# Value projection of the retention by seven products with stationary tokens, and the retention in a staggered, written-out order

## The chip, the cores and the metric

The kernel runs on one core of a Trainium2 chip. The metric is the time of one execution on the device, in microseconds. The work is spread over TensorE (PE in the rows: the matmuls; PEld its weight loads), VectorE (DVE), ScalarE (ACT), GpSimd (POOL), and SyncE (SP), which here only issues DMAs; ScalarE issues the stores, in its own order of instructions.

## What is computed

One decoder layer over 1024 tokens of 1024 channels. The part that the change touches is the retention branch: four heads with keys of 128 and values of 256 channels, in chunks of 128 tokens.

```python
h = rms_norm(x, norm_mix[l])
proj = h @ w_in[l]
aq, ak, av, rq, rk, rv, rg, ga, gr = jnp.split(proj, offsets, axis=-1)
...
def step(state, inp):
    qi, ki, vi = inp
    scores = jnp.einsum('bihd,bjhd->bhij', qi, ki) * decay_intra
    o = jnp.einsum('bhij,bjhv->bihv', scores, vi)
    o = o + jnp.einsum('bihd,bhdv->bihv', qi, state) * decay_q
    state = decay_chunk * state + jnp.einsum('bjhd,bjhv->bhdv', ki * decay_k, vi)
    return state, o
...
ret = head_group_norm(ret, ret_gn_gain[l]).astype(x.dtype) * jax.nn.silu(rg)
merged = jax.nn.sigmoid(ga) * (att @ w_att_o[l]) + jax.nn.sigmoid(gr) * (ret @ w_ret_o[l])
x = x + merged @ w_out[l]
h = rms_norm(x, norm_ffn[l])
x = x + (jax.nn.silu(h @ w_gate[l]) * (h @ w_up[l])) @ w_down[l]
```

`rv` is a product of 1024 tokens, 1024 channels in and 1024 out (four heads of 256); `k` is scaled by `dk ** -0.5` = 128 ** -0.5.

## The kernel before

The activations lie with channels on the partitions and tokens along the free side, in tiles of 128 x 512 (`ut`, 70 of them in a ring; a tile is free again when its last reader is done). Each float32 operand is split into a high and a low part (`split`: a cast on ScalarE, a difference `low` on VectorE), and a product is three matmuls, high x high, high x low, low x high (`mm3`). The normalized input is held in `hT` as high and low parts without the tokens' root mean square; `bc1` (a row per token, spread over the partitions) and `rn` (a column per token) put that in behind the product. Results land in eight banks of PSUM: four of `bank`, four of `abank`.

The stages follow one another: attention's projections and attention itself, with the gate projections `gr` and part of `ga` as filler; then the rest of `ga`, interleaved with attention's output product `ao` (`wo`, `m1`); then the retention; then rg, the product with `w_ret_o`, and the merge; the o stage; and the feed-forward part. The order on TensorE is the order in which the program is written, everywhere. In the feed-forward part, in the o stage and in the merge the other engines' order is written out too; in the stages from the start to rg it is made by a scheduler from what is ready.

The o stage already computes its product (merged with `w_out`) by seven products in place of eight: operands are cut into quarter blocks, sums of blocks (`four_sums`; for the weights `weight_sums`, stored in `d_WS`) are made ahead and stored, and seven products of 4 steps with 12 matmuls each (`o_mm`, `o_evac`), in the order of `STAGES`, reload them a few steps ahead.

Of the retention, the rows name these. `rqk_chunk` makes q or k of one head for 512 tokens (24 matmuls of 512 columns, weights stationary). `rv_chunk` makes the values of one head for 256 tokens: 2 x 8 x 3 = 48 matmuls of 256 columns with the tokens stationary, evacuated as high and low part (`rvh` on ScalarE, `rvl` on VectorE). One **unit** is one head and half of the tokens: `r1` (transposes `pk`, scores `rs`; `kn`, `sT`, `qd` on the other engines), `r2a` (state matmuls `rst`, the states and their parts `shl`), `r2b` (outputs `ro`, their statistics `bst`, `mv`, a root on GpSimd, the normalized `y`), `r3` (transposes `yt`, stored in `d_on`). All q, k and v of head 0 come first; then the units run, and between their steps a chunk of the next head's q, k, v fills TensorE, in the last head the first eight chunks of rg:

```python
for half in range(NH):
    r1(h, half)
    fl.pop(0)()
    r2a(h, half)
    fl.pop(0)()
    r2b(h, half)
    fl.pop(0)()
```

## Time and profile before

| what | value |
|---|---|
| runs | 1482.34, 1483.69 and 2457.64 us, median 1483.69 |
| profiled execution | 1482.5 us |
| its span in the trace | 1480.7 us |
| TensorE, VectorE, ScalarE, GpSimd busy | 1462.5, 972.3, 551.8, 105.8 us |
| matmuls | 7284 |
| DMA | 218.65 MB, mean 148 GB/s |

The span is what lies between the first and the last instruction; the execution's time is 1.8 us more. Busy times of different engines lie beside each other. A matmul's own time overlaps that of the next.

### The profile page before, as it was taken

How to read it: one execution, taken by the hardware profiler on the slowest of the kernel's cores; microseconds unless marked ns; L12 is line 12 of the kernel's file. 1: busy time of each engine (PE TensorE's matmuls, PEld its weight loads, DVE VectorE, ACT ScalarE, POOL GpSimd, SP SyncE). 2: the span in 40 equal slices, each digit the busy share in tenths (PEclk: the TensorE clock that was granted, in tenths of full speed). 3: DMA queues.
4: the chain of work that ended last, by engine and by line, in shares of the span. 5: the costliest groups of instructions: out<-in, count | busy, mean ns of one | idle time of the engine just before them, and what ended most of it. 6: DMA issues, size and time to landing. Idle time of an engine off the chain costs nothing.

```text
span 1480.7 us, 19756 instructions
## 1 busy us (share of the span) xinstructions
PE 1462.5 (99%) x7284; PEld 1239.5 (84%) x7284; DVE 972.3 (66%) x1762; ACT 551.8 (37%) x1055; POOL 105.8 (7%) x108
## 2 busy tenths in 40 slices
PE   9999999999999999999999999999999999999997
PEld 6888888888998998888878778888888888888887
DVE  5888876433445546634579798876667777568774
ACT  6554453211223324332255553222333325444441
POOL 6200000000010010000012300000000000010121
PEclk9999999999999999999999999999999999999999
DMA  5222114453112113345689334432334546799773
GB/s 198 87 66 71 64 44 137 145 166 124 46 45 72 44 43 99 115 147 187 234 275 328 101 104 152 136 124 103 106 126 157 172 161 208 259 323 369 222 234 110
DMA packets 108258, 218.65 MB, mean 148 GB/s; under 512 B 12225, under 2 KB 22593, under 8 KB 108161
## 3 DMA queue, kind: packets, MB, share of 16 engines
q1 hardware_dynamic: 77088, 161.91, 33.8%
q10 hardware_dynamic: 30656, 54.67, 10.0%
q8 instruction: 57, 0.93, 0.3%
q0 software_dynamic: 416, 0.81, 0.2%
q14 instruction: 41, 0.33, 0.1%
HBM read 158.88 MB, written 58.46 MB: 147 GB/s over the span
## 4 chain that ended last, share of the span: by engine, by line
PE 90%; DVE 5%; DMA 2%; issue 2%; ACT 1%; SPq 0%; POOL 0%; POOLq 0%; DVEq 0%; ACTq 0%
PE d L932 14%; PE fu L932 13%; PE fg L932 12%; PE o L932 3%; PE rv_p L102 2%; PE rv_p L104 2%; PE rv_p L103 2%; PE rg_p L102 2%; PE rg_p L103 2%; PE ga_p L102 2%; PE ga_p L103 2%; PE ga_p L104 2%; PE rg_p L104 2%; PE ro_p L102 2%; PE ro_p L103 2%; PE ro_p L104 2%
## 5 line engine op out<-in xcount | busy, mean ns | idle before, releaser
L128 POOL TENSOR_TENSOR ssq<-ssq,sq 128x512 f32<-128x512 f32 x39 | 61.1, 1566 | 788.3 <-DMA rt<-d_X 460.6
L102 PE MATMUL rv_p<-wrv_h,z_h 128*128 128x256 f32 x256 | 72.9, 285 | 0.0
L104 PE MATMUL rv_p<-wrv_h,z_l 128*128 128x256 f32 x256 | 72.4, 283 | 0.0
L103 PE MATMUL rv_p<-wrv_l,z_h 128*128 128x256 f32 x256 | 72.4, 283 | 0.0
L102 PE MATMUL gr_p<-z_h,wgr_h 128*128 128x512 f32 x128 | 50.7, 396 | 0.0
L102 PE MATMUL rg_p<-z_h,wrg_h 128*128 128x512 f32 x128 | 50.2, 392 | 0.0
L102 PE MATMUL ga_p<-z_h,wga_h 128*128 128x512 f32 x128 | 50.0, 391 | 0.0
L103 PE MATMUL gr_p<-z_l,wgr_h 128*128 128x512 f32 x128 | 49.9, 390 | 0.0
L104 PE MATMUL gr_p<-z_h,wgr_l 128*128 128x512 f32 x128 | 49.9, 390 | 0.0
L103 PE MATMUL ga_p<-z_l,wga_h 128*128 128x512 f32 x128 | 49.8, 389 | 0.0
L104 PE MATMUL rg_p<-z_h,wrg_l 128*128 128x512 f32 x128 | 49.8, 389 | 0.0
L103 PE MATMUL rg_p<-z_l,wrg_h 128*128 128x512 f32 x128 | 49.8, 389 | 0.0
L104 PE MATMUL ga_p<-z_h,wga_l 128*128 128x512 f32 x128 | 49.8, 389 | 0.0
L102 PE MATMUL ro_p<-reh,wro_h 128*128 128x512 f32 x128 | 49.8, 389 | 0.0
L103 PE MATMUL ro_p<-rel,wro_h 128*128 128x512 f32 x128 | 49.8, 389 | 0.0
L104 PE MATMUL ro_p<-reh,wro_l 128*128 128x512 f32 x128 | 49.8, 389 | 0.0
L103 PEld LDWEIGHTS rv_p<-wrv_l,z_h 128*128 128x128 f32 x256 | 49.1, 192 | 0.0
L102 PEld LDWEIGHTS rv_p<-wrv_h,z_h 128*128 128x128 f32 x256 | 49.1, 192 | 0.0
L104 PEld LDWEIGHTS rv_p<-wrv_h,z_l 128*128 128x128 f32 x256 | 49.1, 192 | 0.0
L974 ACT ACTIVATE fg_c<-fg_c 128x512 f32<-128x512 f32 x33 | 20.9, 633 | 71.7 <-DVE fg_c L1016 43.6
L852 ACT CAST fg_w_h<-fg_s 128x512 fp32r<-128x512 f32 x44 | 26.9, 619 | 53.2 <-PE fu L932 49.6
L852 ACT CAST fu_w_h<-fu_s 128x512 fp32r<-128x512 f32 x44 | 26.7, 615 | 45.4 <-PE fu L932 21.3
(1540 smaller groups left out, 4596.7 us busy)
## 6 DMA issues: line engine op xcount, KB each, us to landing
dr<-in_w_down_dram SPq DMA_DIRECT2D x56, 256.0 KB, 4.7
d_X<-fg_c ACTq DMA_DIRECT2D x44, 256.0 KB, 3.3
rt<-d_X SPq DMA_DIRECT2D x44, 256.0 KB, 4.5
x<-in_xT_dram SPq DMA_DIRECT2D x32, 256.0 KB, 5.4
rb<-d_X SPq DMA_DIRECT2D x32, 256.0 KB, 3.9
dr<-d_S SPq DMA_DIRECT2D x24, 256.0 KB, 4.0
fg_rb<-in_w_gate_dram SPq DMA_DIRECT2D x11, 512.0 KB, 4.0
fu_rb<-in_w_up_dram SPq DMA_DIRECT2D x11, 512.0 KB, 3.8
```

The source lines that it names most:

```text
L102: nc.tensor.matmul(ps, lhsT=wh, rhs=xh, start=start, stop=False)
L103: nc.tensor.matmul(ps, lhsT=wh, rhs=xl, start=False, stop=False)
L104: nc.tensor.matmul(ps, lhsT=wl, rhs=xh, start=False, stop=stop)
L128: nc.gpsimd.tensor_tensor(out=acc, in0=acc, in1=sq, op=ALU.add)
L852: nc.scalar.copy(out=hi, in_=src)
L932: nc.tensor.matmul(ps, lhsT=w[a][:, c], rhs=x, start=start and j == 0 and i == 0, stop=stop and j == len(xs) - 1 and i == 2, skip_group_ch ...
L974: nc.scalar.activation(s, t, AF.Silu)
```

## The change

The value projection is made once for all heads, as one product of 1024 x 1024 x 1024 by seven products of quarter blocks in the manner of the o stage. The tokens are the stationary side, 512 columns of weights move: 7 products x 4 blocks of 128 tokens x 4 blocks of channels x 3 = 336 matmuls of 512 columns (`h_mm`, 28 steps of 12).

- **Preparation**, in the stage of ga and ao: `h_in` loads x again (16 tiles), `h_blocks` normalizes them on VectorE, forms sums by `four_sums` and stores all seven kinds of blocks in `d_H`; `sums_load` and `sums_add` form the sums of the value weights (now laid out as quarters, `w_mix`) into `d_WM`. The sums of `w_out`, which stood there, move into the last 16 half-runs of rg.
- **q and k of head 0** come before the seven products (`rqk_p`), and are stored (`d_qk`) and loaded again.
- **The seven products** reload blocks (`h_load`, `hw_raw`), cut them (`h_hi`, `h_lo`, `hw_hi`, `hw_lo`), and add results up (`h_evac`); the values go to `d_v`. What each step of work is given ahead stands in a table `hat` by step.
- **The retention** gets its values from `d_v` (`r0`, cut in `r0v`). Its units are staggered: state matmuls of unit u, fill, output transposes of u-1, fill, scores of u+1, outputs of u, two fills. A fill is half a run of q, k (heads 1 to 3) or rg, 12 matmuls of 512 columns (`two_runs`, `pop`). The order on VectorE, ScalarE, GpSimd and SyncE is written out from here on as well. The states have five buffers in place of two, `ro` lies in `bank`, the products of rg with the retention's outputs are made later (`rg_fin`, `rg_end`), and `wro0` is loaded four half-runs before the end.
- The scale of k moves into the constants.

```diff
+    d_H = dr.tile([7, KD // 2, P, HT], F32, name="d_H")
+    d_WM = dr.tile([KD // 2, 4, P, HT], F32, name="d_WM")
+    d_qk = dr.tile([2, NH, P, HT], F32, name="d_qk")
+    d_v = dr.tile([NB, 2, P, HT], F32, name="d_v")
...
+    SUMS = ((1, 0, 1, 0), (0, 0, 2, 2), (2, 1, 2, 1), (3, 2, 3, 3))
+
+    def sums_load(src, name):
+        t = [ut(f"{name}{i}") for i in range(4)]
+        for i in range(4):
+            nc.sync.dma_start(t[i], src[:, i * 512:(i + 1) * 512])
+        return t
+
+    def sums_add(t, dst, i, put=None):
+        o, x, y, n = SUMS[i]
+        nc.vector.tensor_tensor(out=t[o], in0=t[x], in1=t[y], op=ALU.add)
+        (put or (lambda f: f()))(lambda: store(dst[n], t[o]))
+
+    def weight_sums(src, dst, name):
+        t = sums_load(src, name)
...
+    def h_in(j):
+        for r in range(2):
+            for c in range(NH):
+                t = ut(f"hn{2 * j + r}{c}")
+                nc.sync.dma_start(t, xv[2 * j + r, c])
+                HB_[j, r, c] = t
+
+    def h_blocks(j):
+        B_ = {}
+        for r in range(2):
+            for c in range(NH):
+                t = HB_.pop((j, r, c))
+                nc.vector.scalar_tensor_tensor(out=t, in0=t, scalar=gmix_s[:, 2 * j + r:2 * j + r + 1], in1=bc1[c],
+                                               op0=ALU.mult, op1=ALU.mult)
+                B_[r, c] = t
+        put = lambda q, t, d=0: store(d_H[QN.index(q), j], t)
+        for q, rc in (("b11", (0, 0)), ("b21", (1, 0)), ("b22", (1, 1))):
+            put(q, B_[rc])
+        HR["b11", j] = B_[0, 0]
+        h_hi("b11", j)
+        h_lo("b11", j)
+        one, two = four_sums(lambda r, c: B_[r, c], put, lambda i: ut(f"h{i}s{j}"))
+        two(one())
...
+    def hw_raw(k, i):
+        t = wp.tile([P, 1024], F32, tag="raw", name=f"hw{k}{i}_r", bufs=2)
+        if k in (1, 2, 4):
+            c = {1: 2, 2: 3, 4: 1}[k] * HT
+            src = w_mix[i:i + 2, :, c:c + HT]
+        else:
+            src = d_WM[i:i + 2, {5: 0, 6: 1, 7: 2, 3: 3}[k]]
+        nc.sync.dma_start(t.rearrange("p (i c) -> p i c", i=2), src.rearrange("i p c -> p i c"))
...
+    def h_mm(k, q, i):
+        if k not in (2, 3):
+            HB[{1: 2, 5: 3}.get(k, k), i] = HB[k, i] = (bank if k in (1, 5) else abank)(f"h{k}_{i}")
+        ps = HB[k, i]
+        ts = slice(i * P, (i + 1) * P)
+        for j in range(NJ):
+            xh, xl = HX[q][j]
+            wh, wl = HW[k, j][:2]
+            for n, (x, w) in enumerate(((xh, wh), (xh, wl), (xl, wh))):
+                nc.tensor.matmul(ps, lhsT=x[:, ts], rhs=w, start=k not in (2, 3) and j == 0 and n == 0,
+                                 stop=j == NJ - 1 and n == 2, skip_group_check=True)
...
+    def h_evac(k, i):
+        tt = nc.vector.tensor_tensor
+        ps = HB[k, i]
+        if k in (1, 2):
+            t = ut(f"hc{k}{i}")
+            nc.scalar.copy(out=t, in_=ps)
+            if k == 1:
+                HN[i] = t
+            else:
+                h_keep(0, 0, i, t)
+        elif k == 6:
+            tt(out=HN[i], in0=ps, in1=HN[i], op=ALU.subtract)
+        elif k == 7:
...
+    h_in(0)
+    NGB = 2 * KD
     for b in range(KD):
         for half in range(NH):
-            if 2 * b + half >= NGA:
+            if NGA <= 2 * b + half < NGB:
                 ga_chunk(b, half)
             if half == 0:
                 wo = wload(w_att_o[b], f"wao{b}")
@@ -484,44 +638,152 @@
             m1 = ut(f"m1{b}{half}")
             nc.vector.tensor_tensor(out=m1, in0=po, in1=SG.pop((b, half)), op=ALU.mult)
             store(d_m1[b, half], m1)
-        if b % 2:
-            weight_sums(b // 2)
-
-
+            if half == 0 and b % 2 == 0:
+                h_blocks(b // 2)
+            if half == 0 and b % 2 == 1 and b // 2 + 1 < NJ:
+                h_in(b // 2 + 1)
+            if half == 1 and b % 2 == 0:
+                WQ = sums_load(w_mix[b // 2], f"wq{b}")
+            if half == 0 and b % 2 == 1:
+                for i in range(4):
+                    sums_add(WQ, d_WM[b // 2], i)
+    for i, u in enumerate((U_RQ, U_RK)):
+        w = wload(w_in[u], f"wr{i}")
+        for half in range(NH):
+            ps = proj_half(w, hT, half, KD, f"rqk_p{i}{half}")
+            t = ut(f"rqk{i}{half}")
+            times_rstd(t, ps, half)
+            store(d_qk[i, half], t)
+            if i:
+                hw_raw(1, 2 * half)
+                for j in (2 * half, 2 * half + 1):
+                    hw_hi(1, j)
+                    hw_lo(1, j)
...
+    hsteps, hat = [], {}
+
+    def hahead(k, f):
+        hat.setdefault(max(k, 0), []).append(f)
+
+    for n, (k, q) in enumerate(STAGES):
+        for i in range(4):
+            t = 4 * n + i
+            if n > 0:
+                if i % 2 == 0:
+                    hahead(4 * n - 6 + i // 2, lambda a=(k, i): hw_raw(*a))
+                hahead(4 * n - 3 + i // 2, lambda a=(k, i): hw_hi(*a))
+                hahead(4 * n - 2 + i // 2, lambda a=(k, i): hw_lo(*a))
+                hahead(4 * n - 8 + i, lambda a=(q, i): h_load(*a))
+                hahead(4 * n - 6 + i, lambda a=(q, i): h_hi(*a))
+                hahead(4 * n - 5 + i, lambda a=(q, i): h_lo(*a))
+            hsteps.append((lambda a=(k, q, i): h_mm(*a), lambda a=(k, i): h_evac(*a)))
...
+            wat.setdefault(i - 8, []).append(lambda: w_in_raw(key, b, w_in[unit + b]))
+            wat.setdefault(i - 3, []).append(lambda: w_in_cut(key, b))
+
+        def run(a):
+            if a == 0:
+                run.ps = bank(f"{key}_p{b}{half}")
+            wh, wl = W[key, b][:2]
+            for k in range(4 * a, 4 * a + 4):
+                c = slice(k * P, (k + 1) * P)
+                mm3(run.ps, wh[:, c], wl[:, c], *hT[k][half], k == 0, k == KD - 1)
+            if a:
+                use(b, half, run.ps)
+
+        fl.extend([lambda: run(0), lambda: run(1)])
...
+    def rg_use(b, half, ps):
+        s = ut(f"srg{b}{half}")
+        times_rstd(s, ps, half)
+        soon.append(lambda: nc.scalar.activation(s, s, AF.Silu))
+        RS[b, half] = s
+
+    def rg_fin():
+        for b, half in [x for x in RS if (x[0] // 2, x[1]) in RD]:
+            s = RS.pop((b, half))
+            on = ut(f"onr{b}{half}")
+            nc.sync.dma_start(on, d_on[b, half])
+            later.append((2, lambda s=s, on=on, b=b, half=half: rg_end(s, on, b, half)))
+
+    def rg_end(s, on, b, half):
+        nc.vector.tensor_tensor(out=s, in0=s, in1=on, op=ALU.mult)
+        hl = ut(f"reh{b}{half}", F32R), ut(f"rel{b}{half}", F32R)
+        nc.scalar.copy(out=hl[0], in_=s)
+        later.append((1, lambda: low(hl[1], s, hl[0])))
+        ret[b][half] = hl
...
+    def retention_fill():
+        for h in range(1, 4):
+            for w, u in (("q", U_RQ), ("k", U_RK)):
+                for half in range(NH):
+                    two_runs("r" + w, u, h, half, rqk_use(w))
+        for c in range(2 * KD):
+            two_runs("rg", U_RG, c // 2, c % 2, rg_use)
+
...
+    def r0(h, half):
+        for i, w in enumerate("qk"):
+            if h == 0:
+                t = ut(f"r{w}{h}{half}")
+                nc.sync.dma_start(t, d_qk[i, half])
+                RT[w, h, half] = t
+        for c2 in (2 * half, 2 * half + 1):
+            t = ut(f"rv{h}{c2}")
+            nc.sync.dma_start(t.rearrange("p (t c) -> p t c", t=2),
+                              d_v[2 * c2:2 * c2 + 2, h // 2, :, (h % 2) * 256:(h % 2 + 1) * 256].rearrange("t p c -> p t c"))
+            RT["v", h, c2] = t
+
+    def r0v(h, half):
+        for c2 in (2 * half, 2 * half + 1):
+            hl = ut(f"rvh{h}{c2}", F32R), ut(f"rvl{h}{c2}", F32R)
+            split(RT["v", h, c2], *hl)
+            RT["v", h, c2] = hl
 
...
+    un = [(h, half) for h in range(4) for half in range(NH)]
+    NR = len(fl)
...
+    WS_ = []
+    for m in range(4):
+        wat.setdefault(NR - 16 + 3 * m, []).append(wm_sums(m))
+        for i in range(4):
+            wat.setdefault(NR - 16 + 3 * m + 2 + i // 2, []).append(
+                lambda m=m, i=i: sums_add(WS_[m], d_WS[m], i, lambda f: later.append((1, f))))
+    wat.setdefault(NR - 4, []).append(lambda: MWRO.append(wload(w_ret_o[0], "wro0")))
+    MWRO = []
...
+    def pop(n=1):
+        for _ in range(n):
+            i = ran[0]
+            ran[0] += 1
+            due = [f for d, f in later if d <= 1]
+            later[:] = [(d - 1, f) for d, f in later if d > 1]
+            for f in due + wat.pop(i, []):
+                f()
+            if fl:
                 fl.pop(0)()
-            r3(h, half)
-            if h < 3:
-                fl.pop(0)()
-    for f in rest[8:]:
-        f()
...
+    r0(*un[0])
+    r0(*un[1])
+    pop()
+    r0v(*un[0])
+    pop()
+    r1(*un[0])
+    pop(2)
+    for u in range(len(un)):
+        if u + 2 < len(un):
+            r0(*un[u + 2])
+        r2a(*un[u])
+        if u + 1 < len(un):
+            r0v(*un[u + 1])
+        pop()
+        if u > 0:
+            r3(*un[u - 1])
+            RD.add(un[u - 1])
+        pop()
+        if u + 1 < len(un):
+            r1(*un[u + 1])
+        rg_fin()
+        r2b(*un[u])
+        pop(2)
+    pop(1)
+    r3(*un[-1])
+    RD.add(un[-1])
+    rg_fin()
+    while fl:
+        pop(1)
+        rg_fin()
+    while later or wat:
+        pop()
+    hman.close()
 
...
+        dt[:, h] = np.where(diff >= 0, np.exp(lg * np.maximum(diff, 0.0)), 0.0) * P ** -0.5
         dq[:, h] = np.exp(lg * (idx + 1.0))[None, :]
-        dk[:, h] = np.exp(lg * (P - 1.0 - idx))
+        dk[:, h] = np.exp(lg * (P - 1.0 - idx)) * P ** -0.5
```

TensorE where the value projection begins, before (names: `z` channels of the normalized input, `wrk`, `wrv` weights, `_h` and `_l` high and low part):

```order
L102 MATMUL rk_p01_3337<-z71_h_356,wrk0_h_3305 128x512
L103 MATMUL rk_p01_3337<-z71_l_357,wrk0_h_3305 128x512
L104 MATMUL rk_p01_3337<-z71_h_356,wrk0_l_3306 128x512
L102 MATMUL rv_p00_3376<-wrv00_h_3365,z00_h_135 128x256
L103 MATMUL rv_p00_3376<-wrv00_l_3366,z00_h_135 128x256
L104 MATMUL rv_p00_3376<-wrv00_h_3365,z00_l_136 128x256
L102 MATMUL rv_p00_3376<-wrv00_h_3365,z10_h_144 128x256
```

And TensorE at the same place now (`hw` weights, `Hb11` the first block of tokens and channels, `h1_0` the bank of the first product's first token block):

```order
L107 MATMUL rqk_p11_3468<-z71_l_361,wr1_h_3427 128x512
L108 MATMUL rqk_p11_3468<-z71_h_360,wr1_l_3428 128x512
L595 MATMUL h1_0_3535<-hw10_h_3462,Hb110h_2579 128x512
L595 MATMUL h1_0_3535<-hw10_l_3463,Hb110h_2579 128x512
L595 MATMUL h1_0_3535<-hw10_h_3462,Hb110l_2580 128x512
L595 MATMUL h1_0_3535<-hw10_h_3462,Hb111h_2700 128x512
L595 MATMUL h1_0_3535<-hw10_l_3463,Hb111h_2700 128x512
```

Ahead of the projection stand q and k of head 0 in both, and the moving side of a matmul of the projection is now 512 columns in place of 256.

SyncE's queue in the stage of ga and ao, before (`wao`, `wga` weights of ao and ga, `ws` quarters of `w_out`):

```order
L86 DMA wga3_r_2696<-in_w_in_dram 128x1024
L86 DMA wao3_r_2730<-in_w_att_o_dram 128x512
L86 DMA wga4_r_2812<-in_w_in_dram 128x1024
L471 DMA ws00_2614<-in_w_out_dram 128x512
L471 DMA ws01_2615<-in_w_out_dram 128x512
```

And SyncE's queue in the same stage now (`hn` the x loaded again, `wq` quarters of the value weights):

```order
L528 DMA hn30_2643<-in_xT_dram 128x512
L528 DMA hn31_2645<-in_xT_dram 128x512
L90 DMA wga4_r_2882<-in_w_in_dram 128x1024
L90 DMA wao4_r_2916<-in_w_att_o_dram 128x512
L509 DMA wq20_2758<-in_w_mix_dram 128x512
```

wga4 stood behind wao3; now twelve loads of hn and wq, of which the last two are shown, have moved between them.

VectorE in the first unit of the retention, from its first state on, before (`wrq2` weights of q of head 2, `bst` the statistics of `ro`):

```order
L568 COPY state00_3662<-rst000_3655 128x256
L570 SCALAR_TENSOR_TENSOR state01_3667<-state00_3662,rst000_3655 128x256
L77 TENSOR_TENSOR shl00_3664<-state00_3662,shl00_3664 128x256
L570 SCALAR_TENSOR_TENSOR state02_3679<-state01_3667,rst001_3672 128x256
L77 TENSOR_TENSOR shl01_3669<-state01_3667,shl01_3669 128x256
L570 SCALAR_TENSOR_TENSOR state03_3684<-state02_3679,rst001_3672 128x256
L77 TENSOR_TENSOR shl02_3681<-state02_3679,shl02_3681 128x256
L77 TENSOR_TENSOR shl03_3686<-state03_3684,shl03_3686 128x256
L239 TENSOR_TENSOR rq11_3714<-rq_p11_3689,bc11_118 128x512
L77 TENSOR_TENSOR wrq2_l_4221<-wrq2_r_4219,wrq2_h_4220 128x1024
L596 BN_STATS bst0000_3728<-ro000_3716 128x6
L596 BN_STATS bst0001_3731<-ro000_3716 128x6
```

And VectorE at the same place now (`rvl` the low part of the values of the unit that follows):

```order
L831 COPY state00_4297<-rst000_4290 128x256
L833 SCALAR_TENSOR_TENSOR state01_4299<-state00_4297,rst000_4290 128x256
L833 SCALAR_TENSOR_TENSOR state02_4308<-state01_4299,rst001_4301 128x256
L833 SCALAR_TENSOR_TENSOR state03_4310<-state02_4308,rst001_4301 128x256
L81 TENSOR_TENSOR shl00_4312<-state00_4297,shl00_4312 128x256
L81 TENSOR_TENSOR shl01_4314<-state01_4299,shl01_4314 128x256
L81 TENSOR_TENSOR shl02_4316<-state02_4308,shl02_4316 128x256
L81 TENSOR_TENSOR shl03_4318<-state03_4310,shl03_4318 128x256
L81 TENSOR_TENSOR rvl02_4325<-rv02_4186,rvh02_4324 128x512
L81 TENSOR_TENSOR rvl03_4329<-rv03_4188,rvh03_4328 128x512
L81 TENSOR_TENSOR wrq2_l_4192<-wrq2_r_4190,wrq2_h_4191 128x512 x2
L243 TENSOR_TENSOR rk10_4365<-rk_p10_4336,bc10_121 128x512
```

The four states stand together, their low parts behind them, and then the low parts of the next unit's values, which came from the value projection's evacuation before; the statistics of `ro` come after the next unit's scores.

## Rows read from the trace of the kernel before

**Rows 1.** The profile's page: engines' busy time, and the chain that ended last
```profile
PE 1462.5 (99%) x7284; PEld 1239.5 (84%) x7284; DVE 972.3 (66%) x1762; ACT 551.8 (37%) x1055; POOL 105.8 (7%) x108
...
PE 90%; DVE 5%; DMA 2%; issue 2%; ACT 1%; SPq 0%; POOL 0%; POOLq 0%; DVEq 0%; ACTq 0%
```

**Rows 2.** Windows by stage: busy us (instructions) of five engines, clock, DMA share, GB/s
```profile
245.00:343.60 98.60, 98.60 (x436) 81.64 (x435) 37.84 (x50) 17.88 (x24) 0.00 (x0) 1.00 0.48 157
...
365.40:441.60 76.20, 76.20 (x554) 72.23 (x553) 34.11 (x70) 20.39 (x36) 6.26 (x10) 1.00 0.14 44
441.60:562.00 120.40, 120.40 (x839) 112.45 (x838) 60.52 (x127) 35.75 (x63) 12.50 (x20) 1.00 0.18 57
562.00:705.00 143.00, 143.00 (x678) 120.00 (x677) 75.62 (x130) 46.57 (x76) 4.99 (x9) 1.00 0.42 138
...
746.00:816.00 70.00, 69.00 (x310) 56.44 (x309) 60.47 (x91) 36.88 (x64) 13.51 (x9) 1.00 0.91 313
```

**Rows 3.** Costliest groups of the page: busy us, mean ns of one, idle before
```profile
L102 PE MATMUL rv_p<-wrv_h,z_h 128*128 128x256 f32 x256 | 72.9, 285 | 0.0
...
L102 PE MATMUL rg_p<-z_h,wrg_h 128*128 128x512 f32 x128 | 50.2, 392 | 0.0
```

**Rows 4.** Timeline of TensorE at three places: start us, length us, instruction
```profile
354.49 0.39 PE L102 MATMUL rk_p<-z_h,wrk_h 128*128 128x512 f32 x1
...
365.37 0.28 PE L102 MATMUL rv_p<-wrv_h,z_h 128*128 128x256 f32 x1
...
388.41 0.60 PE L535 MATMUL pk<-ident,rk 128*128 128x128 f32 x4
388.84 1.06 PE L538 MATMUL rs<-rq,rk 128*128 128x128 f32 x8
...
395.21 0.28 PE L102 MATMUL rst<-rvh,kn_h 128*128 128x256 f32 x1
...
410.10 1.04 PE L613 MATMUL yt<-ident,y 128*128 128x128 f32 x8
```

**Rows 5.** Groups of VectorE and ScalarE in the o stage, 746 to 816 us
```profile
L77 DVE TENSOR_TENSOR ow_l<-or,ow_h 128x512 fp32r<-128x512 f32 x26 | 19.7, 767 | 5.4 <-ACT ow_h L852 5.2
...
L852 ACT CAST ow_h<-or 128x512 fp32r<-128x512 f32 x24 | 14.8, 620 | 8.1 <-DMA or<-in_w_out_dram 5.5 <-DMA or<-d_WS 1.3
...
L793 ACT COPY on<-o 128x512 f32<-128x512 f32 x4 | 2.3, 584 | 0.0
```

**Rows 6.** Timeline of ScalarE: the issue of one store on its queue
```profile
742.89 0.33 ACTq L246 DMA_DIRECT2D d_M<-m1r  x1
```

**Rows 7.** Waits in the o stage: total us, times, longest us
```profile
ACT Mt41h L746 <- DMA mrt<-d_M: 2.4, 1, 2.4
...
PE o L932 <- DVE Mb213l L77: 0.5, 1, 0.5
```

**Rows 8.** Groups of VectorE in the retention, 441 to 562 us
```profile
L603 DVE TENSOR_SCALAR y<-ro,mv,rs 128x256 f32<-128x256 f32 x16 | 8.0, 540 | 7.6 <-POOL rs L600 7.6
L596 DVE BATCH_NORM_STATS2 bst<-ro 128x6 f32<-128x256 f32 x16 | 6.4, 413 | 0.9 <-PE ro L104 0.9
L77 DVE TENSOR_TENSOR shl<-state,shl 128x256 fp32r<-128x256 f32 x14 | 5.7, 421 | 1.3 <-ACT shl L80 0.9
...
L77 DVE TENSOR_TENSOR sTl<-sT,sTh 128x512 fp32r<-128x512 f32 x4 | 2.8, 692 | 2.7 <-ACT sTh L80 2.7
...
L597 DVE BATCH_NORM_AGGREGATE mv<-bst 128x2 f32<-128x6 f32 x16 | 2.6, 170 | 0.1
```

**Rows 9.** Waits in the retention, 441 to 562 us
```profile
DVE y L603 <- POOL rs L600: 7.6, 8, 1.1
```

**Rows 10.** DMA issues, 700 to 816 us, and all: KB, us to landing
```profile
mrt<-d_M SPq DMA_DIRECT2D x16, 256.0 KB, 5.3
or<-d_WS SPq DMA_DIRECT2D x16, 256.0 KB, 5.2
...
wga_r<-in_w_in_dram SPq DMA_DIRECT2D x8, 512.0 KB, 3.6
```

More of the change, by code (lines that the diff above doesn't have):

```diff
@@ new lines, in trunk, with four_sums, one, two @@
+    STAGES = list(zip((1, 2, 6, 7, 4, 5, 3), QN))
+    held, now, lowq = [], [0], []
+    NJ = KD // 2
+    def four_sums(get, put, names):
+        def one():
+            t1, t3 = names(1), get(0, 1)
+            nc.vector.tensor_tensor(out=t1, in0=get(0, 0), in1=t3, op=ALU.subtract)
+            nc.vector.tensor_tensor(out=t3, in0=t3, in1=get(1, 1), op=ALU.subtract)
+            put("t1", t1, 2)
+            put("t3", t3, 2)
+            return t1
+        def two(t1):
+            t2, t4 = names(2), get(1, 0)
+            nc.vector.tensor_tensor(out=t2, in0=get(1, 1), in1=t1, op=ALU.add)
+            nc.vector.tensor_tensor(out=t4, in0=t4, in1=t2, op=ALU.subtract)
+            put("t2", t2, 2)
+            put("t4", t4, 2)
+        return one, two
@@ new lines, in hw_hi, with hw_lo @@
+    def hw_hi(k, i):
+        nc.scalar.copy(out=HW[k, i][0], in_=HW[k, i][2])
+    def hw_lo(k, i):
+        hi, lo, raw = HW[k, i]
+        low(lo, raw, hi)
+    def h_mm(k, q, i):
[9 more added lines that the diff above has]
+                                 stop=j == NJ - 1 and n == 2, skip_group_check=True)
@@ new lines, in trunk @@
+    for k, (mm, evac) in enumerate(hsteps):
+        now[0] = k
+        if k == len(hsteps) - 6:
+            retention_fill()
+        for f in [f for i in sorted(wat) if i <= k - len(hsteps) for f in wat.pop(i)]:
+            f()
+        for f in hat.get(k, []):
+            f()
+        mm()
+        evac()
+        due = [f for d, f in held if d <= k]
+        held[:] = [(d, f) for d, f in held if d > k]
+        for f in due:
+            f()
+    for _, f in held:
+        f()
+    held.clear()
@@ L572, in r2a @@
                 RT["state", h] = new
-                shl = rp.tile([P, 512], F32R, tag="shl", name=f"shl{h}{c}", bufs=5)
-                split(new, shl[:, :256], shl[:, 256:])
-                RT["sh", h, c + 1] = shl
+                new_.append((c, new))
+        for c, new in new_:
+            shl = rp.tile([P, 512], F32R, tag="shl", name=f"shl{h}{c}", bufs=5)
+            nc.scalar.copy(out=shl[:, :256], in_=new)
+            RT["sh", h, c + 1] = shl
+        for c, new in new_:
+            shl = RT["sh", h, c + 1]
+            low(shl[:, 256:], new, shl[:, :256])
     def r2b(h, half):
```

191 lines of the change are left out of this document (82 added, 109 removed).

## The prediction

> **What bounds the kernel now.** I read the page first. TensorE is busy 1462.5 us, 99% of the span, and the chain that ended last is TensorE for 90% [rows 1]. So time is saved only where TensorE gets less to do, and lost only where it is made to wait. The windows by stage come next: from 245 to 705 us, which holds nearly everything that the change rewrites, TensorE is busy for the whole of each window, at the full granted clock [rows 2]. There is no stall here for a better order to remove.
>
> How long a matmul takes must not be read from its mean duration. The mean is 285 ns for one of 256 columns and 392 ns for one of 512 [rows 3], but they overlap, and only the spacing of the starts costs time. From 354.49 to 365.37 us stand the 2 x 24 = 48 matmuls of 512 columns of rk: 10.88 / 48 = 0.2267 us each. From 365.37 to 388.41 us stand the first 4 x 48 = 192 of rv: 23.04 / 192 = 0.1200 us each [rows 4].
>
> **The products.** The value projection goes from 4 heads x 4 token pairs x 48 = 768 matmuls of 256 columns to 7 products x 4 token blocks x 12 = 336 of 512 columns. Before: 768 x 0.1200 = 92.2 us. After: 336 x 0.2267 = 76.2 us. The gain is **16.0 us**, all of it on the path. Of it 10.2 us are the eighth of the moved columns that the seven products save (24,576 columns at the slope of the two spacings, 0.1067 us for 256), the other 5.8 us are the 432 matmuls fewer at the fixed 13.3 ns that the same two spacings leave. All other matmuls (q, k, rg, the retention's own) keep number and shape, and only change place.
>
> A rule of the Trainium skill speaks of this sum. The spacings above are 0.1200 and 0.2267 us [rows 4]. "TensorE: Matmul & The Clock Gate", section "Back-to-back issue gap", gives N/2.4 + 2.5 ns between single matmuls at the full clock, so 109.2 and 215.8 ns. By that the sum would be 83.8 - 72.5 = 11.3 us, 4.7 us less gain; the rows differ from the page, and the sum goes by the rows.
>
> **The stage of the seven products (28 steps of 12 matmuls, 2.72 us each).** Its feed is new: per stage four blocks of d_H come back, two 512 KB weight loads come in, all are cut into high and low parts, and the products are added up. VectorE gets 24 low parts of reloaded blocks, 24 of weights and 20 sums: 68 x 0.69 to 0.77 us [rows 5, 8] = 47 to 52 us of 76.2. ScalarE gets 48 casts x 0.62 and 8 copies x 0.58 [rows 5], and 16 stores at 0.33 us [rows 6]: 40 us. The transfers are 24 x 0.25 + 12 x 0.5 + 16 x 0.25 = 16 MB, some 220 GB/s. The nearest thing in the trace is the o stage, built the same way: there VectorE is busy 60.5 of 70 us, the DMA moves 313 GB/s, and TensorE still idles only 1.0 us [rows 2], the longest time 0.5 us for a low part, where ScalarE had waited 2.4 us at a time for reloads [rows 7]. The new stage is lighter in both. Bounds: 0 (nothing late) and 2.0 us (twice the o stage's idle, for reloads that also wait for their stores); I take 0.8, near the o stage's 1.0, because the plan of steps is the same.
>
> **The retention.** TensorE needs per unit: 12 state matmuls 1.44 us (395.21 on at 0.12 [rows 4]), 48 fill matmuls 10.88, 24 of ro 2.88, transposes 1.04 and scores some 1.3 (0.43 between their starts and 1.06, less what overlaps [rows 4]): 17.5 us. VectorE's share of a unit by [rows 8]: y 4 x 0.540, bst 4 x 0.413, mv 4 x 0.170, the states and their low parts 8 x 0.42, and ten of 512 columns (kn, sT, its low part, that of qd, two of v, two evacuations, two weight halves) at 0.69: 14.8 us, and about 1 us of waiting for GpSimd's root (7.6 us in 8 waits [rows 9]). That is 15.8 of 17.5 us, where before VectorE had 60.5 of 120.4 us over nearly four units [rows 2]: the stage is shorter by the rv matmuls that used to lie between. In the last two units rg's ends come on top: two products and two low parts, 4 x 0.69 = 2.8 us, together 18.6, over 17.5. The order eases it: from the state matmuls to the ro that needs them stand 7.8 us of TensorE work (two fills, transposes, scores) against 3.4 us of states, and the scores' chain has ro and two fills, 8.3 us, for its 2.8 us plus what VectorE has queued. VectorE's order is now written out, so where it waits for GpSimd the next evacuation waits behind it, and TensorE runs on only as long as the four banks last. Bounds: 0 below (a gain is excluded, since there is no idle time now) and 8 us (three late units at 2.7 us: 18.6 - 17.5 = 1.1, and the root's wait and one evacuation once more, 1.0 + 0.69, where the order makes VectorE stand for them). I take 1.5 us, nearer zero, since four banks cover over 10 us of fill and only two of eight units are above.
>
> **The preparation in the ga and ao stage.** Here 16 loads of x, 16 scalings, 16 sums, 8 cuts and 28 stores are added, while the sums of w_mix take the place of those of w_out one for one. On VectorE that is 36 operations at 0.69 to 0.77 us [rows 5, 8] = 25 to 28, so 63 to 66 us of 98.6 [rows 2]; on ScalarE 28 x 0.33 + 4 x 0.62 = 12 us to its 17.9. 44 transfers of 256 KB are 11.5 MB, which lifts 157 GB/s to some 275, under the o stage's 313 [rows 2]. TensorE has hundreds of matmuls of ga and ao as cover. What is queued behind the new loads on SyncE's queue is wga4 (the order above): the loads wait for free tiles, and whatever they wait the next weights wait too, and ga's first matmul behind them. A weight load lands in 3.6 us [rows 10] and is asked for one column block ahead, about 16 us. Bounds: 0 and 5 us; I take 0.5, since the room for it is large.
>
> **The rest.** Weight sums of w_out go to the last 16 half-runs of rg, where 32 more transfers of 8 MB fall into some 38 us; the DMA share there is 0.42 now [rows 2]. The cost is hidden by rg's matmuls; without that cover the o stage's first or<-d_WS would be late by a landing, 5.2 us [rows 10]. The wro0 load comes some 10 us earlier, worth 0 to 1 us. I take +0.3 for both, bounds -1 and 3. q and k of head 0 move from one stage into the same place, cost 0; the scale of k in the constants is free.
>
> **Sum.** -16.0 + 0.8 + 1.5 + 0.5 + 0.3 = -12.9 us. The profiled execution took 1482.5 us for its 1480.7 us of span; it becomes 1469.6. The median of the runs shown, 1483.69 us, is 1.2 above the profiled one and the fastest, 1482.34, is 0.2 below; I predict **1470 us**. 2% of the median, about what a measurement of this kernel can tell from no change, is 29.7 us: 1454.0 to 1513.4 counts as no difference.
>
> **Rivals.**
> 1. *The busy time is what counts.* If the 768 matmuls really cost 0.285 us and the 336 ones 0.39, the change is worth 219 - 131 = 88 us, so 1395 us, faster. For it: the page's busy column. Against it: the starts in [rows 4], and TensorE's busy share of 99% with every stretch summing to its own length. Chance 0.01.
> 2. *VectorE becomes the bound in the retention.* Its 15.8 of 17.5 us leave 1.7 us a unit, and with the order fixed a late evacuation holds up the next unit. At the upper bound of 8 us instead of 1.5 the time is 1476.5; with the two other new stages at their bounds as well, 1481.8. For it: 18.6 over 17.5 in two units. Against it: the bank cover. Chance 0.17.
> 3. *The reloads come too late, slower.* Every stage of the seven products (after the first, which uses blocks still held) rests on two raw weight tiles: the second load of a stage can go out only once the low part of the one before it is made, about 4.5 steps ahead and used 0.5 step into its stage, 5 x 2.72 = 13.6 us. Less 2.6 us for two casts and two low parts, and one step of queueing on the fixed orders, about 8.3 us remain for the landing. The landings are 5.2 and 5.3 us in the o stage, 3.6 for 512 KB weights where there is less traffic [rows 10]. It pays back all the gain where each of six stages loses 16.0 / 6 = 2.7 us, that is at a landing of 11 us; at twice the o stage's 5.3 plus the wait of a store on which it rests, 14 us, six stages lose 34 us and the kernel takes 1501 us, slower than before though within 2%. At 17 us it would pass 1513. Chance 0.05, of it 0.02 beyond 2%.
> 4. *The preparation delays the gate's weights*, each of four column blocks by 3.2 us beyond its cover: all gain gone, 1483. Against it: 16 us of lead. Chance 0.04.
>
> **How the numbers follow.** The forecast, 1464 to 1475, has 0.73. Rivals 1 to 4 have 0.01, 0.17, 0.05 and 0.04. The best case is all new terms at zero and wro0's 1 us: 1482.5 - 17 = 1465.5, with a spread of the runs of 1 to 2 us downward: low end 1464. The high end takes in rival 2 with its neighbours at their bounds, 1481.8 for the profiled execution, and the 1.2 us of the median: 1483. Left out are rival 1, 3, most of 4 and what may be left over of the forecast, together under 0.15. Faster by over 2% only by rival 1, and some unseen gain: 0.02. Slower by over 2%: 0.03. Within 2%: 0.95.
>
> **What the profile of after would show.** Starts of the h matmuls 0.227 us apart and 76 to 78 us from the first to the last; no idle TensorE there, or waits for a low part (Ht, hw) of under 1 us. If idle time is named after DMA hw or hr on ScalarE, rival 3 is at work. Retention units 17.5 us long, VectorE at 0.85 to 0.95 in them, any TensorE wait released by shl, kn or an evacuation in the last two units (rival 2). TensorE idle before a ga matmul, released by wga, is rival 4. I am wrong if the span falls by less than 7 us, or if the matmul spacing of the h products is not that of the other 512-column ones (their stationary side is the tokens, as rv's was, and not the weights, as rk's).

## The result, and the profile after

The changed kernel takes 1465.84 us (median of 4 runs, 1465.27 to 1467.86), the kernel before 1483.01 (4 runs): a ratio of 0.9888, 95% interval 0.9869 to 0.9908. One of those four executions took 2457.64 us and pulls their median up; the other three have the median 1482.34, so the gain by the medians is 16.5 us, clear of the noise and below the 2% that counts as a difference here. The profiled execution took 1465.27 us; its span is 1463.5, 17.2 us less than the 1480.7 before.

The page of the changed kernel, beside [rows 1]: engines' busy time, then the chain that ended last.

```profile
PE 1445.8 (99%) x6852; PEld 1208.5 (83%) x6852; DVE 1037.6 (71%) x1876; ACT 576.0 (39%) x1109; POOL 104.6 (7%) x108
...
PE 91%; DVE 5%; issue 2%; ACT 1%; DMA 1%; SPq 0%; POOL 0%; POOLq 0%; DVEq 0%; ACTq 0%
```

TensorE's busy time fell by 16.7 us and its share of the span is 99% as before, while VectorE took on 65 us. The 432 matmuls fewer (7284 to 6852) are those that were forecast, and no engine has come to stand beside TensorE in the chain.

The windows by stage of the changed kernel, with the columns of [rows 2]: ga and ao; q and k of head 0; the seven products; the retention; rg; the o stage.

```profile
245.00:343.30 98.30, 98.30 (x436) 81.38 (x435) 60.25 (x88) 19.74 (x29) 0.00 (x0) 1.00 0.81 277
343.30:365.10 21.80, 21.80 (x98) 18.06 (x97) 3.96 (x6) 1.11 (x2) 0.00 (x0) 1.00 0.59 170
365.10:441.30 76.20, 76.20 (x338) 63.10 (x337) 44.59 (x70) 31.71 (x58) 1.60 (x2) 1.00 0.66 221
441.30:560.00 118.70, 118.70 (x689) 104.04 (x688) 88.48 (x192) 47.97 (x89) 19.95 (x31) 1.00 0.31 98
560.00:690.00 130.00, 130.00 (x617) 109.09 (x615) 82.32 (x144) 46.08 (x77) 3.71 (x8) 1.00 0.64 216
...
731.00:801.00 70.00, 69.66 (x314) 57.30 (x313) 62.44 (x93) 38.28 (x66) 13.91 (x9) 1.00 0.88 308
```

From 245 to 690 us, where nearly all of the change lies, TensorE is busy for the whole of each window: nothing of what was added there held it up. The load is visible all the same: VectorE went from 37.8 to 60.3 us in the ga stage, the DMA from 157 to 277 GB/s.

TensorE's timeline at the first and the last of the seven products' matmuls, with the columns of [rows 4]:

```profile
364.83 0.39 PE L108 MATMUL rqk_p<-z_h,wr_l 128*128 128x512 f32 x1
365.06 0.39 PE L595 MATMUL h<-hw_h,Hb110h 128*128 128x512 f32 x1
365.28 0.39 PE L595 MATMUL h<-hw_l,Hb110h 128*128 128x512 f32 x1
...
440.99 0.39 PE L595 MATMUL h<-hw_h,Hb223l 128*128 128x512 f32 x1
441.21 0.39 PE L106 MATMUL rq_p<-z_h,wrq_h 128*128 128x512 f32 x1
```

From 365.06 to 441.21 us: 76.15 us for 336 matmuls, 0.2266 us each, the spacing of rk before. A matmul still lasts 0.39 us by its own row.

The part that was rewritten begins with the first matmul of q of head 0 and ends before the first with `w_ret_o`. Before:

```profile
343.61 0.39 PE L102 MATMUL rq_p<-z_h,wrq_h 128*128 128x512 f32 x1
...
659.64 0.39 PE L102 MATMUL ro_p<-reh,wro_h 128*128 128x512 f32 x1
```

and now:

```profile
343.30 0.39 PE L106 MATMUL rqk_p<-z_h,wr_h 128*128 128x512 f32 x1
...
643.43 0.39 PE L106 MATMUL ro_p<-reh,wro_h 128*128 128x512 f32 x1
```

That is 316.03 us before and 300.13 now, 15.9 less. Of the other 1.3 us of the span's 17.2, 0.3 lie ahead of this part and 1.0 in the o stage, whose program is the same in both.

### The profile page after: what moved, and what is told of

It reads as the page before. It is cut to its first block, busy times and chain, and to the rows that moved or that the text cites. A ratio compares the mean times of both kernels' runs of the same rounds, so it can differ in the third digit from the quotient of the medians.

```text
span 1463.5 us, 19401 instructions
## 1 busy us (share of the span) xinstructions
PE 1445.8 (99%) x6852; PEld 1208.5 (83%) x6852; DVE 1037.6 (71%) x1876; ACT 576.0 (39%) x1109; POOL 104.6 (7%) x108
## 4 chain that ended last, share of the span: by engine, by line
PE 91%; DVE 5%; issue 2%; ACT 1%; DMA 1%; SPq 0%; POOL 0%; POOLq 0%; DVEq 0%; ACTq 0%
PE d L500 14%; PE fu L500 13%; PE fg L500 13%; PE h L595 5%; PE o L500 4%; PE rg_p L106 2%; PE ga_p L106 2%; PE rg_p L108 2%; PE rg_p L107 2%; PE ga_p L108 2%; PE ro_p L108 2%; PE ro_p L107 2%; PE ga_p L107 2%; PE ro_p L106 2%; PE gr_p L106 2%; PE gr_p L108 2%
## 5 line engine op out<-in xcount | busy, mean ns | idle before, releaser
L81 DVE TENSOR_TENSOR dw_l<-dr,dw_h 128x512 fp32r<-128x512 f32 (+1 forms) x48 | 33.8, 708 | 11.6 <-ACT dw_h L1120 11.6
L1120 ACT CAST dw_h<-dt 128x512 fp32r<-128x512 f32 (+1 forms) x36 | 21.1, 586 | 52.7 <-DVE dt L1431 45.0
L372 ACT ACTIVATE st<-st,nm 128x128 f32<-128x128 f32 x64 | 25.0, 391 | 32.3 <-DVE nm L364 29.1
L1431 DVE TENSOR_TENSOR dt<-dr 128x512 f32<-128x512 f32 (+1 forms) x36 | 25.8, 715 | 15.0 <-DMA dr<-in_w_down_dram 14.9
L990 DVE TENSOR_TENSOR sgr<-ro_p,sgr 128x512 f32<-128x512 f32 x16 | 11.0, 690 | 34.2 <-PE ro_p L108 33.9
L1120 ACT CAST dw_h<-dr 128x512 fp32r<-128x512 f32 (+1 forms) x48 | 27.8, 584 | 17.6 <-DMA dr<-in_w_down_dram 7.5
```

What stands on the lines that cost most here:

```text
L81: (eng or nc.vector).tensor_tensor(out=out, in0=raw, in1=hi.bitcast(F32), op=ALU.subtract)
L372: nc.scalar.activation(st[:, c], st[:, c], AF.Exp, bias=nm[:, j:j + 1], accum_out=sb[:, 4 * n2 + j:4 * n2 + j + 1])
L990: nc.vector.tensor_tensor(out=sg, in0=MT[b, half], in1=sg, op=ALU.mult)
L1120: nc.scalar.copy(out=hi, in_=src)
L1431: nc.vector.tensor_tensor(out=t, in0=r[0], in1=r[i], op=ALU.add)
```

## The experiments

All are the changed kernel, edited as shown. The table has medians of several executions, in the order of their time; ratio and interval are against the kernel before on the same chip.

| kernel | median us | ratio to before, 95% interval |
|---|---|---|
| changed kernel | 1465.84 | 0.9888, 0.9869 to 0.9908 |
| sched | 1467.19 | 0.9899, 0.9884 to 0.9914 |
| dve_4 | 1467.59 | 0.9892, 0.9874 to 0.9910 |
| slots_68 (one run) | 1468.88 | none |
| h_256 | 1471.39 | 0.9927, 0.9913 to 0.9942 |
| slots_66 | 1472.71 | 0.9925, 0.9911 to 0.9940 |
| no_stagger | 1472.71 | 0.9937, 0.9922 to 0.9952 |
| hn_twice | 1473.51 | 0.9938, 0.9922 to 0.9954 |
| raw_late | 1474.72 | 0.9952, 0.9935 to 0.9968 |
| hn_dram | 1478.14 | 0.9967, 0.9954 to 0.9980 |
| dve_6 | 1478.50 | 0.9966, 0.9953 to 0.9978 |
| no_stagger_sched | 1479.18 | 0.9973, 0.9962 to 0.9983 |
| dve_8 | 1487.91 | 1.0034, 1.0023 to 1.0046 |

Profiled executions differ by up to some 2 us in the first 40 us and by about 1 us each in the o stage and the feed-forward part, also where an edit leaves these alone. So each verdict goes by the length of the edited stage in the trace, and the median stands beside it.

### What a matmul costs: h_256

```diff
-                nc.tensor.matmul(ps, lhsT=x[:, ts], rhs=w, ...)
+                for c in (slice(0, 256), slice(256, 512)):
+                    nc.tensor.matmul(ps[:, c], lhsT=x[:, ts], rhs=w[:, c], ...)
```

> Each of the 336 matmuls of 512 columns of the seven products is split into two of 256 columns, all else as in the changed kernel. Theory A (the time is the spacing of the starts: 0.1067 us for 256 columns and 13.3 ns for every matmul): 336 matmuls more at 13.3 ns, +4.5 us, so 1470.3 us, the stage 672 x 0.1200 = 80.6 us long instead of 76.2. Theory B (only the moved columns cost): no change, 1465.8 us, the stage 76.2 us. Theory C (the mean durations of 284 and 389 ns cost): 672 x 0.284 - 336 x 0.389 = +60 us, 1526 us.

The values that this kernel computes are not the layer's; number and place of all other work stay. The windows of the seven products in this kernel, and in the changed one:

```profile
365.05:445.68 80.63, 80.63 (x673) 80.63 (x672) 45.61 (x70) 31.79 (x58) 1.63 (x1) 1.00 0.62 209
```

```profile
365.06:441.21 76.15, 76.15 (x337) 63.06 (x336) 44.59 (x70) 31.71 (x58) 1.53 (x1) 1.00 0.66 221
```

80.63 us for 672 matmuls is 0.1200 each, 4.48 us more than 76.15 (4.5 forecast, 336 x 13.3 ns). Theories B and C fall. With that the gain divides into two steps: from 92.2 us (768 times the 0.1200 measured before) to 80.63 for seven products in place of eight at the same width, 11.6 us; from 80.63 to 76.15 for the width, 4.5 us.

### Is the feed of the seven products near the path: raw_late

```diff
-        t = wp.tile([P, 1024], F32, tag="raw", name=f"hw{k}{i}_r", bufs=2)
+        t = wp.tile([P, 1024], F32, tag="hraw", name=f"hw{k}{i}_r", bufs=1)
...
-                    hahead(4 * n - 6 + i // 2, lambda a=(k, i): hw_raw(*a))
-                hahead(4 * n - 3 + i // 2, lambda a=(k, i): hw_hi(*a))
-                hahead(4 * n - 2 + i // 2, lambda a=(k, i): hw_lo(*a))
+                    hahead(4 * n - 4 + i, lambda a=(k, i): hw_raw(*a))
+                hahead(4 * n - 3 + i // 2 * 2, lambda a=(k, i): hw_hi(*a))
+                hahead(4 * n - 2 + i // 2 * 2, lambda a=(k, i): hw_lo(*a))
...
-NSLOT = 70
+NSLOT = 69
```

> In the seven products the raw weights have one tile instead of two, so that a load starts only when the load before it has been cut, about one step ahead of its own cut instead of three (and the ring of tiles has 69 instead of 70). Theory A (the reload chain is near the path, the cover of some 8 us carries it): the second load of a stage lands 4 to 5 us after its start, its parts are late by 1 to 2 us in each of six stages, +6 to +12 us, 1472 to 1478 us, with idle time of TensorE before an h matmul released by hw_l. Theory B (the reserve is larger than that): under 1 us, 1466 us.

The window of the stage in this kernel, then the longest of its waits for a weight load (total us, times, longest):

```profile
367.23:449.06 81.83, 78.91 (x337) 62.67 (x336) 44.98 (x70) 31.64 (x58) 1.29 (x1) 1.00 0.65 212
```

```profile
ACT hw_h L580 <- DMA hw_r<-d_WM: 26.9, 8, 4.2
DVE hw_l L81 <- ACT hw_h L580: 17.3, 12, 3.7
ACT hw_h L580 <- DMA hw_r<-in_w_mix_dram: 9.5, 3, 4.3
```

The stage grows from 76.15 to 81.83 us, 5.7 us, just under the lower end of theory A. ScalarE now stands up to 4.3 us for a load, VectorE behind ScalarE, and TensorE loses about 1 us in each of six stages. About half of that is idle time (78.91 of 81.83 us are busy), the rest matmuls that last longer. Of the 9 us by the medians the other 3 lie in the first 40 us (2.2 in the trace) and in the feed-forward part (1.1); whether the tile fewer in the ring has a share in that was not separated. So rival 3 names a real chain, and two raw tiles, asked for three steps ahead of their cut, are what keeps it off the path.

### Which order pays: sched, no_stagger, no_stagger_sched

```diff
-    hman.enter_context(tc.manual_schedule(engines={mybir.EngineType.DVE, mybir.EngineType.Activation,
-                                                   mybir.EngineType.Pool, mybir.EngineType.SP}))
```

> The changed kernel with the order on VectorE, ScalarE, GpSimd and SyncE in the seven products and the retention left to the scheduler, TensorE's order unchanged. Theory A (the order on TensorE decides, the others have room): within 2 us of the changed kernel, 1464 to 1468 us. Theory B (the written-out order is needed): stalls of TensorE released by VectorE or by late loads, over 5 us, 1471 us or more.

In no_stagger the loop over units reads as follows (and the call of `r1` for the next unit is gone):

```diff
+        if u > 0:
+            r1(*un[u])
+            pop()
         r2a(*un[u])
...
+        pop()
+        rg_fin()
+        r2b(*un[u])
+        pop()
+        r3(*un[u])
+        RD.add(un[u])
+        pop()
```

> The seven products stay, the units of the retention run one after the other again (scores, fill, state matmuls, fill, outputs, fill, output transposes, fill, with 12 matmuls in a fill). Theory A (the stagger is what lets the thinner fill cover the chains): from the state matmuls to the outputs 3.4 us of VectorE stand against 2.7 us of fill, from the outputs to the transposes 2.3 + 1.0 + 2.2 = 5.5 us against 2.7, so some 4 us of idle TensorE in each of 8 units, +32 us, 1498 us (1485 to 1515). Theory B (the four banks and the fill cover it in any order): 1466 to 1470 us.

no_stagger_sched has both edits.

> The retention's units one after the other and the order on the other engines left to the scheduler. If the idle time without the stagger comes from the length of the chains in a unit, this is within 10 us of the same kernel with the written-out order. If it comes from an order that is bad for unstaggered units, this returns to 1466 to 1475 us.

The windows from the first state matmul to the end of rg, in the changed kernel:

```profile
453.48:643.43 189.95, 189.95 (x1038) 164.33 (x1036) 141.82 (x290) 76.11 (x135) 22.43 (x38) 1.00 0.42 137
```

in sched:

```profile
453.80:643.75 189.95, 189.95 (x1038) 164.37 (x1036) 133.66 (x286) 72.41 (x131) 22.42 (x38) 1.00 0.43 141
```

in no_stagger:

```profile
454.24:650.05 195.81, 194.21 (x1038) 164.60 (x1036) 142.11 (x290) 75.19 (x135) 23.54 (x39) 1.00 0.41 133
```

and in no_stagger_sched:

```profile
455.17:656.69 201.52, 194.55 (x1038) 164.60 (x1036) 134.00 (x286) 72.34 (x131) 23.50 (x39) 1.00 0.40 131
```

With the stagger it makes no difference who orders the other engines: 189.95 us both times, theory A of sched. Without it the same matmuls take 5.9 us more in the written-out order, 11.6 us more in the scheduler's. Both expectations for no_stagger miss: each unit grows, but by 0.6 us and not 4 (17.69 us from one unit's state matmuls to the next one's, 17.11 in the changed kernel). The chain through one unit's outputs in no_stagger, in order of time (start us, us):

```profile
478.83 0.44 DVE bst L866
479.48 0.33 DVE bst L866
480.40 0.72 POOL rs L869
481.18 0.43 issue
481.61 0.55 DVE y L873
482.19 0.77 PE yt L883 x5
```

From the last statistics to the transposes it is 3.4 us, not 5.5: the first bank's statistics and half of the y lie beside other work. Against 2.7 us of fill that leaves 0.7, near the 0.6. no_stagger_sched bears out the first of its two theories, the length of the chains: at 1479.18 us it is within 10 us of no_stagger, and it doesn't come back to 1475 or less. The written-out order even helps there, by 5.7 us. What it says beyond this: with the seven products alone, and the retention ordered nearly as before, the kernel gains 4 us over the kernel before (1479.18 against 1483.22 on the same chip), not 16. sched, which differs from it by the stagger alone, has the other 12.

### When VectorE becomes the bound: dve_4, dve_6, dve_8

```diff
             split(RT["v", h, c2], *hl)
+            for _ in range(N):
+                low(hl[1], RT["v", h, c2], hl[0])
```

with N of 2, 3 and 4, on two tiles in each unit.

> Four operations of 512 columns (0.69 us each, 2.8 us) more on VectorE in each unit of the retention, ahead of the next unit's values (the low parts of the values are made three times). The trace of the changed kernel shows units 17.1 us long with VectorE busy 14.0 to 14.8 us in the first six. Theory A (VectorE has room until its work and its waits fill the unit): 14.4 + 2.8 = 17.2 us plus about 1 us of waits, just over 17.1, so 0 to 1 us per unit, 1466 to 1474 us. Theory B (the reserve is in the places between the steps, each with 3 to 4 us of slack, and is already used up): 2 us or more per unit, 1482 us or more.

> Six operations of 512 columns (4.1 us) more on VectorE in each unit of the retention. With four more TensorE had no idle time, with eight the units grew from 17.1 to 20.1 us. Theory A (VectorE sets the unit when its work exceeds it): 14.4 + 4.1 = 18.5 us against 17.1, so 1.4 us or a little more in 7 units, +10 to +13 us, 1476 to 1479 us. Theory B (the idle with eight came from one late step, which six don't reach): under 3 us, 1469 us or less.

> Eight such operations (5.5 us) more on VectorE in each unit. Theory A: 14.4 + 5.5 + 1 = 20.9 us against 17.1, VectorE sets the unit, 3 to 4 us in each of 7 units, +21 to +28 us, 1487 to 1494 us. Theory B (the banks take it up): under 1470 us.

The windows from the first state matmul to the end of rg, dve_4:

```profile
454.77:644.72 189.95, 189.95 (x1038) 164.35 (x1036) 159.70 (x318) 75.98 (x135) 22.43 (x38) 1.00 0.42 137
```

dve_6:

```profile
453.79:655.20 201.41, 195.67 (x1037) 165.58 (x1036) 169.24 (x333) 75.19 (x135) 22.34 (x38) 0.99 0.39 131
```

dve_8:

```profile
453.74:665.22 211.48, 199.92 (x1037) 166.88 (x1036) 179.93 (x348) 76.19 (x137) 22.28 (x38) 0.98 0.38 126
```

Four operations more per unit cost nothing, six cost 11.5 us, eight cost 21.5: a threshold between four and six, and 10 us more for the last two. Theory A gave 0 to 8, 10 to 13 and 21 to 28, and the result lies inside each time. About half of the loss in dve_8 is idle time (199.92 of 211.48 us are busy); the other 10 us are the same matmuls lasting longer, with a granted clock of 0.98 over the window. dve_8 takes 1487.91 us and is the one kernel that is slower than before: rival 2 is a real mechanism, four to six small operations per unit away from this kernel. TensorE's waits in dve_8 (total us, times, longest) show where it enters:

```profile
PE yt L885 <- DVE y L875: 8.9, 12, 1.6
PE rst L106 <- ACT kn_h L122: 0.7, 1, 0.7
PE rst L108 <- DVE kn_l L123: 0.6, 2, 0.3
```

Most of what is late are the transposes for the normalized outputs. One unit of dve_4, and then three of the changed kernel, by their windows, tell why four are free:

```profile
505.19:522.30 17.11, 17.11 (x103) 15.07 (x101) 15.84 (x34) 6.61 (x12) 3.76 (x6) 1.00 0.20 62
```

```profile
503.90:521.01 17.11, 17.11 (x103) 15.07 (x101) 12.70 (x28) 6.61 (x12) 3.34 (x6) 1.00 0.29 93
...
538.11:555.22 17.11, 17.11 (x102) 15.07 (x101) 11.84 (x27) 8.42 (x14) 2.11 (x6) 1.00 0.23 78
555.22:572.33 17.11, 17.11 (x103) 15.07 (x101) 13.66 (x30) 8.46 (x16) 2.18 (x4) 1.00 0.34 109
```

Over the first seven units of the changed kernel VectorE is busy 91.07 us, 13.0 in each (11.8 to 13.7; the last unit has 15.4), not the 14.8 that I had summed. The 14.0 to 14.8 us in the expectation for dve_4, and the 14.4 in those that follow, are too high in the same way, so theory A's numbers came out partly by luck. The shares show what it left out. Over these seven units VectorE is busy 77% of the time in the changed kernel (91.07 of 118.85 us), 90% in dve_4 (107.31 of 118.85), and 91% in dve_6 (114.05 of 125.17) and in dve_8 alike (124.70 of 136.80): here it doesn't get above about 91%. By an estimate from that, 0.91 x 17.11 - 13.0 = 2.6 us were free in a unit, four operations at 0.60 us, the spacing of their starts in a row (shown with the retention below).

### The preparation: hn_twice, hn_dram, slots_66, slots_68

```diff
                 nc.sync.dma_start(t, xv[2 * j + r, c])
+                nc.sync.dma_start(t, xv[2 * j + r, c])
```

> Each of the 16 loads of x in the stage of ga and ao is issued twice, 4.2 MB more in front of the gate's weights on SyncE's queue. Theory A (the weights asked for one column block ahead, 16 us, take that up): no change, 1465 to 1467 us. Theory B (the preparation's loads delay the gate's weights, which are near the path): idle TensorE before ga matmuls, 3 us or more, 1469 us or more.

TensorE loses 7.1 us in one place, theory B in its size. The chain that leads there, in order of time:

```profile
249.90 0.68 DVE h2s L489
...
250.61 6.86 DMA d_H<-h2s
...
257.49 4.43 DMA hn<-in_xT_dram
...
261.94 6.11 DMA hn<-in_xT_dram
...
268.75 1.22 DVE wga_l L81
...
274.30 0.61 DVE sga L243
...
274.96 0.80 PE ga_p L106
```

A store of a sum has to land before its tile is free for the next x; the x is loaded, and loaded a second time behind the first; VectorE, in its given order, stands for it, and the evacuation of ga (`sga`), which frees TensorE's bank, stands behind it. It was not the load of the gate's weights, as rival 4 had it: SyncE issued it at 247.41 us, ahead of these loads of x, and such a load lands in 3.9 to 4.5 us in this kernel. hn_dram was to tell latency from traffic:

```diff
                 nc.sync.dma_start(t, xv[2 * j + r, c])
+                nc.sync.dma_start(d_ex[2 * j + r, c], xv[2 * j + r, c])
```

> Behind each of the 16 loads of x in the stage of ga and ao stands one more DMA of 256 KB on the same queue, from DRAM to DRAM, into a buffer that nothing reads: the queue position and the traffic of the doubled loads without their second landing, on which VectorE waited in the kernel with the loads doubled (that one had 7.1 us of idle TensorE near 265 us, at the end of a chain store, x load, second x load). Theory A (the chain to VectorE's scalings is what is short of time): under 1 us of idle in this stage, 1465 to 1468 us. Theory B (the traffic or the place ahead of the gate's weights is): 4 to 8 us again, 1470 to 1474 us.

It doesn't tell them apart, and takes longer than either theory had. The sixteen copies wait for nothing, and the scheduler put them to the very start, as SyncE's timeline shows (start us, length us):

```profile
1.64 3.17 SPq L530 DMA_DIRECT2D d_ex<-in_xT_dram  x5
4.85 0.59 SPq L191 DMA_DIRECT2D x<-in_xT_dram  x1
```

Between the loads of x on which everything begins they cost some 12 us (TensorE is busy 29.1 of the first 40 us instead of 36.1, at a granted clock of 0.83 instead of 1.00, and ao begins at 252.0 us instead of 239.9), and in the ga stage nothing. The traffic's part in hn_twice is open.

Two kernels with a smaller ring were to tell whether the tiles are what is short (slots_68 has 68):

```diff
-NSLOT = 70
+NSLOT = 66
```

> The ring of 128 x 512 tiles has 66 instead of 70, all else as in the changed kernel. Theory A (in the stage of ga and ao the loads of x wait for a tile that a store frees, and VectorE stands for them): the loads start some microseconds later, 2 to 6 us of idle TensorE before ga matmuls near 260 us, 1468 to 1474 us. Theory B (the ring has room): under 1 us, 1465 to 1468 us.

> The ring has 68 tiles. Theory A: between the kernels with 70 and 66 tiles, 0 to 3 us of idle TensorE in the stage of ga and ao. Theory B: none.

Neither has any idle TensorE in the ga stage: the ring alone doesn't make the loads of x late, even with four tiles fewer, and theory A falls for that place. What slots_66 loses (6.9 us by the medians, 5.8 by the spans) lies elsewhere: 0.7 us at the start of the product with `w_ret_o`, and most, some 4 us, at one wait in the feed-forward part, of which the waits of TensorE in this kernel show

```profile
PE fu L500 <- ACT fu_p L1263: 3.8, 1, 3.8
```

where the changed kernel has 1.7 us in the same row. In the 20 us around it TensorE starts 58 matmuls here, at a granted clock of 0.83, and 78 in the changed kernel, at 1.00. Why a smaller ring does that is open.

## Why the prediction was right, point by point

The forecast was 1470 us, the result 1465.84, inside the range of 1464 to 1483 but near its low end: the profiled 1465.27 us is what the prediction called its best case, 1465.5. The direction and the term that carries the change were right; the sum is 4 us too high.

**What bounds the kernel** held: this kernel, whose TensorE has no gap there, gives back what is taken from TensorE, 15.9 us in the rewritten part.

**The products**, -16.0 us: 92.2 us, by the spacing before, stand against 76.15 measured, -16.05. This term alone carries the result. Rival 1, the sum by mean durations, would have given 1395 us; in h_256 it would have given +60 us and measured +4.5.

The rule of the Trainium skill beside it, from "TensorE: Matmul & The Clock Gate", section "Back-to-back issue gap", is one for isolated matmuls at the full clock (109.2 and 215.8 ns); the estimate by it was a gain of 11.3 us. The spacings of the h matmuls, which stand in a stream, are 120.0 ns at 256 columns and 226.6 at 512, so the trace has other numbers, and the measurement decides.

**The stage of the seven products**, +0.8 us: 0. Its load was forecast well (VectorE 47 to 52 us, measured 44.6; 220 GB/s, measured 221). The o stage was the wrong yardstick for the stall: it idles with VectorE at 86% and 313 GB/s, while this stage, at 59% and 221, doesn't. Which of the two makes the difference is not shown. raw_late shows that the chain of rival 3 is there.

**The retention**, +1.5 us, and rival 2: 0. The step that failed is VectorE's 14.8 us per unit and the 18.6 against 17.5 in the last two units. They measure 13.0 us on average, and 13.7 and 15.4 in the last two, in units of 17.11; nor does any y wait for GpSimd's root any more, for which the sum had 1 us. I had summed mean durations, the very thing that I had refused to do for TensorE. VectorE's timeline in the changed kernel (start us, length us):

```profile
262.87 0.69 DVE L481 TENSOR_TENSOR h1s<-hn,hn 128x512 f32<-128x512 f32 x1
263.47 0.69 DVE L81 TENSOR_TENSOR wao_l<-wao_r,wao_h 128x512 fp32r<-128x512 f32 x1
264.07 0.68 DVE L482 TENSOR_TENSOR hn<-hn,hn 128x512 f32<-128x512 f32 x1
```

Operations that last 0.69 us start every 0.60; at that ratio 14.8 becomes 12.9. The room is between four and six operations wide, as dve_4 and dve_6 bracket it.

**The preparation**, +0.5 us, and rival 4: 0 as the kernel stands. hn_twice shows a price of some microseconds for this stage, but at another place than rival 4 has it: at VectorE's order and not at the weights' queue.

**The rest**, +0.3 us: 0 in rg and at wro0. The 1.3 us that the span lost outside the rewritten part I don't credit to the change: the o stage idles 0.3 us here, 1.0 us in [rows 2], and 1.0 us again in sched, whose o stage is the same program.

```profile
731.30:801.30 70.00, 68.98 (x311) 56.63 (x310) 61.66 (x92) 37.67 (x65) 13.76 (x9) 1.00 0.88 309
```

So all four stall terms, 3.1 us together, measured zero, and the products measured what the spacing said. Two smaller sums of the prediction are off: rival 2's 1476.5 us is reckoned from the rounded 1470 and its 1481.8 from 1469.6, so the first should be 1476.1; and rival 3's 1501 us leaves out the other stall terms. The forecast rests on neither. What the prediction did not see is how much the order mattered: it argued that there was no stall for an order to remove, true of the kernel before, while without the stagger the new kernel would have lost 6 to 12 us. That the stagger was there is what made the retention's term zero, and the prediction gave it only the words "the order eases it".
